# The delta-rule stage of a hybrid decoder step: 0/1 sums in two fp32r passes, zero-padded sample products, masks on the way out of PSUM, 32-row state updates

## The chip, the cores and the metric

The kernel runs on one core of a Trainium2 chip. The metric is the device time of one execution in microseconds; less is better. The times shown are medians of several runs of the same program.

## What is computed

One inference step of a decoder layer serves 256 prompt tokens of one request and 64 sample tokens (8 requests of 8 tokens). The layer is a mixer of 8 gated delta-rule heads and 4 retention heads, then attention over 256 memory tokens, then a gated feed-forward of 5632 hidden units; the model has 2048 features. All arrays are 32-bit floats. The change touches the delta-rule heads alone. For one head (keys and values of 128 features), in chunks:

```python
def gated_delta_chunked(q, k, v, g, beta, s0):
    # S_t = a_t S_{t-1} + b_t k_t (v_t - a_t S_{t-1}^T k_t)^T,  o_t = S_t^T q_t,  g = log a
    G = jnp.cumsum(g, -1)
    decay = jnp.exp(jnp.where(causal, G[..., :, None] - G[..., None, :], -jnp.inf))
    lower = jnp.where(strict, beta[..., :, None] * kk * decay, 0.0)        # kk = k k^T
    a_mat = lower + jnp.eye(C)
    rhs = jnp.concatenate([v * beta[..., None], k * (beta * jnp.exp(G))[..., None]], -1)
    sol = lax.linalg.triangular_solve(a_mat, rhs, left_side=True, lower=True, unit_diagonal=True)
    ...
    # per chunk: u = u_c - w_c S;  o = (q e^G) S + (qk * decay) u;  S = S e^{G_last} + (k e^{G_last - G})^T u
```

The prompt starts from a zero state; each of the 8 sample requests has a state of 128 x 128 of its own for every head, which is read, used and written back.

## The kernel before

The tokens are columns (256 of the prompt, 64 of the samples, 320 in all), and a weight tile of 128 x 128 is the stationary operand of TensorE. Every 32-bit weight and activation of a projection is cut into a high and a low fp32r part: ACT makes the high one (line 154, `hi`), VectorE the low one (line 155, `lo`), and TensorE adds three products of 320 columns (lines 234 to 236). The weights come in chunks of 1024 columns over SP's queue, four chunks ahead; a chunk is 24 such products. A product whose operands are not fp32r runs as fp32, which shows as two passes in the trace.

The projections are the bulk work. `weave(small, per)` runs a generator of small work beside it: each step of the generator (up to its `yield`) is queued behind a slice of bulk, and a slice asks for `per` nanoseconds of bulk times the yielded weight (2100 ns here, six groups of three products, or 18 products). The order of the instructions on each engine is written at compile time by the tile scheduler, from program order and its own estimate of when operands are ready; on the chip each engine takes its queue in that order.

The generator `gdn(hp)` treats two heads at a time, four pairs in all, each beside the projections of the next pair (the last beside the first retention head's). Its rows are five units of 128 tokens: two units of prompt tokens for each head, and one unit (number 4) with the 64 sample tokens of both heads. Its steps, with the lines of the profile:

- Line 511: `gin`, a triangle of ones times the log decays, on VectorE; it shares four slots (tag `t5`) with `DT`, `DM`, `Nt` and `Nm`. Line 542: inverse norms `r10` on POOL, then `vr` on VectorE (544).
- Lines 550 and 551: `pD` and `pC`, the sums of log decays between two tokens, as fp32 products of a 0/1 matrix with `gin`; ACT takes the exponent into `DT`, POOL masks it into `DM`.
- Lines 566 to 570: `pK` = k k^T and `pQ` = k q^T. Line 574: `pR`, sample keys and queries times the old states, in four column groups of 32; ACT copies it into `R` (580).
- Lines 577 and 578: `Nt` on VectorE. Then the inverse of the 8 x 8 diagonal blocks: `Nm` (583), `Nc` (585, a reduction) and `Z` (588) on VectorE; `pB` (592), a 0/1 product with `Z` on TensorE; 14 short instructions into `U8` (604, 605) and `U` (607) on VectorE.
- Line 597: `pS`, products of 0/1 selections `selK` and `selQ` with `R`, which bring the sample products to their rows.
- Line 612: POOL makes three masked copies `Ns` of `Nt`, one for each level of the blocked inverse (blocks of 8, 16 and 32).
- Lines 638 to 671, three levels: `pQ` from `Ns[i]` and `X`, ACT copies it into `Q` (640), `pU` (654), VectorE subtracts it from `U` (655), TensorE transposes `U` (669), ACT copies that into `X` (671).
- In between, the sample states: POOL scales the old states `S0` (646) and spreads `w` over the requests into `wm` (650); TensorE multiplies in four products of 64 rows and 512 columns (661); VectorE adds each to `S0` (663); SP stores the state.

Small products take their PSUM bank from a pool of four (`ps()`), the bulk from another four (`mm()`). SP's queue holds the weight loads, the state loads and the stores in program order.

Of the kernel before, what the change touches and what calls it, by code (L numbers as in the profile page):

```python
# [14 lines left out]
P = 128  # L15
# [3 lines left out]
NB = 8  # L19
# [25 lines left out]
def _constants():  # L45
# [14 lines left out]
    put("lvl", np.stack([(col // (2 * s) == row // (2 * s)) & (col // s > row // s) for s in (8, 16, 32)], 1))  # L60
# [5 lines left out]
    for name, q in (("selK", 0), ("selQ", 1)):  # L66
        s = np.zeros((P, 2, NS))
        for j in range(4):
            for par in range(2):
                for l in range(NL):  # L70
                    s[32 * j + 16 * q + 8 * par + l, par, NL * (2 * j + par) + l] = 1
        put(name, s)
# [32 lines left out]
def tile_hybrid_step(ctx: ExitStack, tc: tile.TileContext, I, O, gamma8):  # L105
# [63 lines left out]
    class Bulk:  # L169
        """The projections as one stream of tensor-engine work, drawn in slices."""  # L170
# [43 lines left out]
    def project(name, srcs, xs, evac, n=NT, kt=KT, banks=None, held=None, start=()):  # L214
        """srcs: weights [128, (k, 256)], two column tiles each; xs() gives (hi, lo) per 128 rows of K."""
# [68 lines left out]
    g5 = mc.tile([P, HP, 5], F32, name="g5")  # L284
    eG = mc.tile([P, HP, 5], F32, name="eG")
# [5 lines left out]
    def rstd_of(accs, width, n=NT):  # L291
        """1 / sqrt(mean over the partitions of the sum of accs + eps), tokens on partitions, one column per 128."""
# [108 lines left out]
    with tc.tile_pool(name="prep", bufs=1, side="right") as pp:  # L401
        xT = pp.tile([P, KT, NT], F32, name="xT")
        nc.sync.dma_start(gT, I["gains"])
        # pieces of x between the chunks of weights that meet them
# [16 lines left out]
        def prep():  # L421
            accs = [pp.tile([P, NT], F32, name=f"acc0{i}") for i in range(2)]
            for f in range(KT):
                o = pp.tile([P, NT], F32, tag="sq0", name="sq0", bufs=6) if f > 1 else accs[f]
                # behind the cuts that the tensor engine waits for
# [23 lines left out]
            # rows: tokens; the sample tokens twice, once per head of a pair  # L449
# [21 lines left out]
            dve.scalar_tensor_tensor(g5, ab, -1.0, al5[:, 0], op0=ALU.mult, op1=ALU.mult)  # L471
            gb = pp.tile([P, HP, 2 * NB], F32, name="gb")
# [28 lines left out]
    def gdn(hp):  # L501
# [8 lines left out]
        gin = gp.tile([P, 5, P], F32, tag="t5", name="gin", bufs=4)  # L510
        dve.tensor_tensor(gin[:, 0:4], bc(cc("triI").unsqueeze(1), [P, 4, P]), bc(g5[:, hp, 0:4].unsqueeze(2), [P, 4, P]), ALU.mult)
        dve.tensor_scalar(gin[:, 4], cc("triIC"), g5[:, hp, 4:5], None, op0=ALU.mult)
# [45 lines left out]
        kq = gp.tile([P, 2, 4, 2, 16], F32, tag="kq", name="kq")  # L558
        for h in range(2):
            for i, t in enumerate((k, q)):  # L560
                pool.tensor_copy(kq[:, h, :, i, :].rearrange("p j (b l) -> p j b l", b=2), t[:, 512 + h * NS : 512 + (h + 1) * NS].rearrange("p (j b l) -> p j b l", b=2, l=NL))
# [9 lines left out]
        pR = ps()  # L571
        for h in range(2):
            for j in range(4):
                pe.matmul(pR[32 * j : 32 * j + 32, h * NP : (h + 1) * NP], kq[:, h, j].rearrange("p i t -> p (i t)"), S0[h][:, 2 * j : 2 * j + 2, :], start=True, stop=True)
# [17 lines left out]
        pe.matmul(pB[:, :NT], cc("b8"), Z.rearrange("p u m c -> p (u m c)"), start=True, stop=True)  # L592
        pS = ps()
        for o, name in ((0, "selK"), (1, "selQ")):
            for h in range(2):
                for par in range(2):
                    pe.matmul(pS[h * NS : (h + 1) * NS, o * P : (o + 1) * P], cc(name)[:, par * NS : (par + 1) * NS], R[:, h, par], start=par == 0, stop=par == 1)
# [11 lines left out]
        Ns = []  # L609
# [7 lines left out]
        rh = gp.tile([P, 2, P], F32, tag="rh", name="rh")  # L617
        rhC = gp.tile([P, P], F32, tag="rhC", name="rhC")
        dve.scalar_tensor_tensor(rhC, un(pS, 0), nG[:, hp, 4:5], vr[:, 4], op0=ALU.mult, op1=ALU.add)
        qSC = gp.tile([P, P], F32, tag="qSC", name="qSC")  # L620
        act.activation(qSC, un(pS, 1), AF.Copy, scale=eG[:, hp, 4:5])
# [66 lines left out]
        def heads_out(lo, hi):  # L688
            """Head norm of every other unit."""
# [10 lines left out]
        def gates_out(lo, hi):  # L700
            """Back to features on partitions, gain and gate."""
# [10 lines left out]
        # prompt: two chunks from a zero state  # L712
# [54 lines left out]
    def ret(h):  # L767
# [8 lines left out]
        # sample keys and values with every group of 32 tokens four times: (high, low) of one meets (high, low) of the other  # L776
# [46 lines left out]
        # scores, transposed: keys on partitions  # L823
# [100 lines left out]
    def residual(name, w, xs, ssq, xg, gain, firsts=2):  # L924
        """x += W^T of the activations, for all columns; the next norm's inputs follow."""
# [414 lines left out]
```

## Time and profile before

| what | value |
| --- | --- |
| median of 3 runs | 2193.51 us (2192.74 to 2194.01) |
| span of the profiled execution, first to last instruction | 2192.0 us |
| instructions in the trace | 36250 |
| mean granted TensorE clock | 0.994 |
| stage of the delta-rule pairs | about 60 to 430 us |

The page gives the profiled execution by its span only; the timed runs lie 1.5 us above that span. Times in the rows are microseconds from the start of the span unless marked ns. A matmul is pipelined: its row shows a duration longer than the distance from its start to the next one's.

### The profile page before, as it was taken

How to read it: one execution, taken by the hardware profiler on the slowest of the kernel's cores; microseconds unless marked ns; L12 is line 12 of the kernel's file. 1: busy time of each engine (PE TensorE's matmuls, PEld its weight loads, DVE VectorE, ACT ScalarE, POOL GpSimd, SP SyncE). 2: the span in 40 equal slices, each digit the busy share in tenths (PEclk: the TensorE clock that was granted, in tenths of full speed). 3: DMA queues.
4: the chain of work that ended last, by engine and by line, in shares of the span. 5: the costliest groups of instructions: out<-in, count | busy, mean ns of one | idle time of the engine just before them, and what ended most of it. 6: DMA issues, size and time to landing. Idle time of an engine off the chain costs nothing.

```text
span 2192.0 us, 36250 instructions
## 1 busy us (share of the span) xinstructions
PE 2148.7 (98%) x14964; PEld 2062.4 (94%) x14964; DVE 1140.1 (52%) x1617; ACT 861.6 (39%) x1338; POOL 292.2 (13%) x326
## 2 busy tenths in 40 slices
PE   8899999999999999999999999999999999999997
PEld 7898988999999999788889999999999999999997
DVE  7667576465565644454455444444444443444455
ACT  6444434343345533344354333333233332333332
POOL 2324143111114100000001110000000000001011
PEclk9999999999999999999999999999999999999999
DMA  7343433365557545788865454545555445545543
GB/s 249 116 137 98 147 119 112 117 203 190 183 197 258 151 145 152 289 296 292 285 206 152 145 150 149 149 149 154 147 152 149 149 140 158 153 147 154 142 148 116
DMA packets 101974, 369.52 MB, mean 169 GB/s; under 512 B 11696, under 2 KB 12464, under 8 KB 99632
## 3 DMA queue, kind: packets, MB, share of 16 engines
q1 hardware_dynamic: 101808, 367.20, 53.0%
q8 instruction: 117, 1.92, 0.4%
q14 instruction: 49, 0.40, 0.1%
HBM read 345.85 MB, written 21.30 MB: 167 GB/s over the span
## 4 chain that ended last, share of the span: by engine, by line
PE 93%; DVE 3%; DMA 1%; ACT 1%; issue 1%; POOL 0%; SPq 0%; POOLq 0%; DVEq 0%; ACTq 0%
PE mm L234 22%; PE mm L236 22%; PE mm L235 22%; PE ps L236 5%; PE ps L234 5%; PE ps L235 5%; PE mm L979 1%; PE mm L981 1%; PE mm L980 1%; DVE lo L155 1%; PE ps L1130 1%; DMA Vs<-in_cache_mem_v_dram 1%; PE ps L661 1%; PE ps L1188 1%; PE ps L1173 1%
## 5 line engine op out<-in xcount | busy, mean ns | idle before, releaser
L234 PE MATMUL mm<-act,hi 128*128 128x320 f32 (+1 forms) x3456 | 1073.9, 311 | 5.9 <-ACT hi L154 5.9
L155 DVE TENSOR_TENSOR lo<-raw,hi 128x1024 fp32r<-128x1024 f32 (+1 forms) x561 | 687.6, 1226 | 728.6 <-ACT hi L154 725.5
L236 PE MATMUL mm<-act,lo 128*128 128x320 f32 (+1 forms) x3456 | 1063.3, 308 | 3.2 <-DVE lo L155 3.2
L235 PE MATMUL mm<-act,hi 128*128 128x320 f32 (+1 forms) x3456 | 1063.5, 308 | 1.4 <-DVE act L255 1.3
L154 ACT CAST hi<-raw 128x1024 fp32r<-128x1024 f32 (+1 forms) x561 | 579.7, 1034 | 871.8 <-PE mm L235 642.7
L234 PEld LDWEIGHTS mm<-act,hi 128*128 128x128 f32 x3456 | 651.0, 188 | 23.3 <-issue 15.4
L236 PEld LDWEIGHTS mm<-act,lo 128*128 128x128 f32 x3456 | 650.7, 188 | 7.2 <-DVE lo L155 4.4
L235 PEld LDWEIGHTS mm<-act,hi 128*128 128x128 f32 x3456 | 651.2, 188 | 4.8 <-issue 2.2
L236 PE MATMUL ps<-act,lo 128*128 128x320 f32 x704 | 217.7, 309 | 0.0
L235 PE MATMUL ps<-act,hi 128*128 128x320 f32 x704 | 217.6, 309 | 0.0
L234 PE MATMUL ps<-act,hi 128*128 128x320 f32 x704 | 217.6, 309 | 0.0
L1013 POOL TENSOR_TENSOR up<-up,ga 128x320 f32<-128x320 f32 x44 | 60.8, 1383 | 768.6 <-DVE up L1012 733.7
L236 PEld LDWEIGHTS ps<-act,lo 128*128 128x128 f32 x704 | 132.2, 188 | 0.0
L235 PEld LDWEIGHTS ps<-act,hi 128*128 128x128 f32 x704 | 132.2, 188 | 0.0
L234 PEld LDWEIGHTS ps<-act,hi 128*128 128x128 f32 x704 | 132.2, 188 | 0.0
L918 POOL TENSOR_TENSOR acc<-acc,sq 128x320 f32<-128x320 f32 x44 | 52.7, 1199 | 507.1 <-ACT sq L917 506.1
L249 ACT CAST act<-up 128x320 fp32r<-128x320 f32 x44 | 20.2, 460 | 96.9 <-POOL up L1013 96.9
L250 DVE TENSOR_TENSOR act<-up,act 128x320 fp32r<-128x320 f32 x44 | 21.7, 492 | 62.3 <-ACT act L249 62.3
L979 PE MATMUL mm<-hi,act 128*128 128x512 f32 x128 | 51.8, 405 | 0.0
L981 PE MATMUL mm<-hi,act 128*128 128x512 f32 x128 | 50.8, 397 | 0.0
L980 PE MATMUL mm<-lo,act 128*128 128x512 f32 x128 | 50.6, 395 | 0.0
L337 DVE SCALAR_TENSOR_TENSOR cy<-pre,cw,cy 128x344 f32<-128x344 f32 x72 | 46.6, 659 | 4.6 <-ACT cy L335 4.1
(334 smaller groups left out, 1450.0 us busy)
## 6 DMA issues: line engine op xcount, KB each, us to landing
raw<-in_w_in_dram SPq DMA_DIRECT2D x127, 512.0 KB, 3.9
raw<-in_w_gate_dram SPq DMA_DIRECT2D x88, 512.0 KB, 3.8
raw<-in_w_up_dram SPq DMA_DIRECT2D x88, 512.0 KB, 3.8
raw<-in_w_down_dram SPq DMA_DIRECT2D x80, 512.0 KB, 3.6
raw<-in_w_out_dram SPq DMA_DIRECT2D x32, 512.0 KB, 4.1
raw<-in_w_mem_q_dram SPq DMA_DIRECT2D x32, 512.0 KB, 3.9
raw<-in_w_mem_k_dram SPq DMA_DIRECT2D x32, 512.0 KB, 5.5
Kt<-in_cache_mem_k_dram SPq DMA_DIRECT2D x32, 512.0 KB, 7.0
```

The source lines that it names most:

```text
L154: act.copy(hi[:, :n], raw[:, :n])
L155: dve.tensor_tensor(lo[:, :n], raw[:, :n], hi[:, :n].bitcast(F32), ALU.subtract)
L234: pe.matmul(o, hi[:, w], xh[:, :n], start=g == 0, stop=False)
L235: pe.matmul(o, hi[:, w], xl[:, :n], start=False, stop=False)
L236: yield 3 * n / 2.4, pe.matmul(o, lo[:, w], xh[:, :n], start=False, stop=g == kt - 1)
L337: dve.scalar_tensor_tensor(cy[:, :CO], pre[:, i : i + CO], cw[:, i, ch : ch + 1], cy[:, :CO], op0=ALU.mult, op1=ALU.add)
L661: pe.matmul(pS, kd[r, 4], wm[r, 4 * half : 4 * half + 4].rearrange("p b v -> p (b v)"), start=True, stop=True)
L918: pool.tensor_tensor(self.accs[0], self.accs[0], sq, ALU.add)
L979: pe.matmul(pv[mt], xh[:, ms], hi[:, w], start=k0 + k == 0, stop=False)
L980: pe.matmul(pv[mt], xh[:, ms], lo[:, w], start=False, stop=False)
L981: yield 640.0, pe.matmul(pv[mt], xl[:, ms], hi[:, w], start=False, stop=k0 + k == KT - 1)
L1013: pool.tensor_tensor(u, u, sg[m], ALU.mult)
```

## The change

The edit is in `gdn` and in what prepares its constants:

- `gin` and `Z` are made twice, from a high and a low fp32r part of `g5` and of `Nc`, and `pD`, `pC` and `pB` become two accumulated fp32r products each with fp32r copies (`tri`) of the 0/1 matrices. `gin` has slots of its own.
- `kz` and `qz` hold the sample keys and queries with each group of eight columns in its place in a row of zeros, so that 32 accumulated products in four column groups write the sample products straight to their rows. `kq`, `pR`, `R`, `selK`, `selQ` and their products go.
- The level products take `Nt` unmasked; the level mask is applied when VectorE takes `pQ` out of PSUM into `Q`, which ACT copied before.
- The state update is made at level 2 in one step: four products of 32 rows and 512 columns into four PSUM banks, and sixteen VectorE instructions that scale the old state and add.

```diff
     put("strict", row > col)
-    put("lvl", np.stack([... & (col // s > row // s) for s in (8, 16, 32)], 1))
+    put("lvl", np.stack([... & (row // s > col // s) for s in (8, 16, 32)], 1))
...
+            act.copy(g5s[0], g5)
+            dve.tensor_tensor(g5s[1], g5, g5s[0].bitcast(F32), ALU.subtract)
+            for i, name in enumerate(("strict", "strictC", "b8")):
+                act.copy(tri[:, i], cc(name))
...
+    kz, qz = (gp.tile([P, 4, P], F32, name=n) for n in ("kz", "qz"))
+    pool.memset(kz, 0.0)
+    pool.memset(qz, 0.0)
...
-        gin = gp.tile([P, 5, P], F32, tag="t5", name="gin", bufs=4)
-        dve.tensor_tensor(gin[:, 0:4], ..., bc(g5[:, hp, 0:4].unsqueeze(2), [P, 4, P]), ALU.mult)
-        dve.tensor_scalar(gin[:, 4], cc("triIC"), g5[:, hp, 4:5], None, op0=ALU.mult)
+        gins = []
+        for g in g5s:
+            gin = gp.tile([P, 5, P], F32R, tag="gin", name="gin", bufs=2)
+            g = g.bitcast(F32)
+            dve.tensor_tensor(gin[:, 0:4], ..., bc(g[:, hp, 0:4].unsqueeze(2), [P, 4, P]), ALU.mult)
+            dve.tensor_scalar(gin[:, 4], cc("triIC"), g[:, hp, 4:5], None, op0=ALU.mult)
+            gins.append(gin)
+        for z, t in ((kz, k), (qz, q)):
+            s = t[:, 512 : 512 + P].rearrange("p (c b l) -> p c b l", b=4, l=NL)
+            pool.tensor_copy(z[:, :, 0:120].rearrange("p c (b x) -> p c b x", x=40)[:, :, :, 0:NL], s[:, :, 0:3])
+            pool.tensor_copy(z[:, :, 120:P], s[:, :, 3])
...
-        pe.matmul(pD, cc("strict"), gin[:, 0:4].rearrange("p u c -> p (u c)"), start=True, stop=True)
-        pe.matmul(un(pC, 0), cc("strictC"), gin[:, 4], start=True, stop=True)
+        for i, gin in enumerate(gins):
+            pe.matmul(pD, tri[:, 0], gin[:, 0:4].rearrange("p u c -> p (u c)"), start=i == 0, stop=i == 1)
+        for i, gin in enumerate(gins):
+            pe.matmul(un(pC, 0), tri[:, 1], gin[:, 4], start=i == 0, stop=i == 1)
...
-        kq = gp.tile([P, 2, 4, 2, 16], F32, tag="kq", name="kq")
-        (four pool.tensor_copy of k and q into kq)
...
-        pR = ps()
-        for h in range(2):
-            for j in range(4):
-                pe.matmul(pR[32 * j : 32 * j + 32, h * NP : (h + 1) * NP], kq[:, h, j]..., S0[h][:, 2 * j : 2 * j + 2, :], ...)
+        pS = ps()
+        for i, z in enumerate((kz, qz)):
+            for b in range(4):
+                for c in range(4):
+                    pe.matmul(pS[32 * c : 32 * c + 32, i * P : (i + 1) * P], z[:, c, 32 * b : 32 * b + 32], S0[c // 2][:, 4 * (c % 2) + b, :], start=b == 0, stop=b == 3)
...
-        act.copy(R.rearrange("p h a v -> p (h a v)"), pR)
+        act.activation(qSC, un(pS, 1), AF.Copy, scale=eG[:, hp, 4:5])
...
-        dve.tensor_tensor(Z, bc(Nc.unsqueeze(2), [P, 5, NL, NL]), bc(d8.unsqueeze(1), [P, 5, NL, NL]), ALU.mult)
+        Ns = split(Nc.rearrange("p u c -> p (u c)"), None, 5 * NL, dst=[...])
+        for t in Ns:
+            Z = gp.tile([P, 5, NL, NL], F32R, tag="Z", name="Z", bufs=2)
+            dve.tensor_tensor(Z, bc(t.bitcast(F32)..., [P, 5, NL, NL]), bc(d8.unsqueeze(1), [P, 5, NL, NL]), ALU.mult)
+            Zs.append(Z)
+        dve.scalar_tensor_tensor(rhC, un(pS, 0), nG[:, hp, 4:5], vr[:, 4], op0=ALU.mult, op1=ALU.add)
         yield 1.5
...
-        pe.matmul(pB[:, :NT], cc("b8"), Z.rearrange("p u m c -> p (u m c)"), start=True, stop=True)
-        pS = ps()
-        (eight pe.matmul of selK and selQ with R into pS)
+        for i, Z in enumerate(Zs):
+            pe.matmul(pB[:, :NT], tri[:, 2], Z.rearrange("p u m c -> p (u m c)"), start=i == 0, stop=i == 1)
...
-        for i in range(3):
-            t = gp.tile([P, 4, P], F32, tag="Ns", name="Ns", bufs=3)
-            pool.tensor_tensor(t, Nt[:, 0:4], bc(lv(i).unsqueeze(1), [P, 4, P]), ALU.mult)
-            Ns.append(t)
...
             for u in range(4):
-                pe.matmul(un(pQ, u), Ns[i][:, u], X[:, u], start=True, stop=True)
+                pe.matmul(un(pQ, u), Nt[:, u], X[:, u], start=True, stop=True)
             Q = gp.tile([P, 4, P], F32, tag="Q", name="Q")
-            act.copy(Q, g4(pQ))
+            dve.tensor_tensor(Q, g4(pQ), bc(lv(i).unsqueeze(1), [P, 4, P]), ALU.mult)
             if i == 0:
...
-                for h in range(2):
-                    pool.tensor_tensor(S0[h], S0[h], bc(eTC[:, hp, h * NB : (h + 1) * NB].unsqueeze(2), [P, NB, P]), ALU.mult)
-                wm = gp.tile([P, NB, P], F32, tag="wm", name="wm")
-                (two pool.tensor_tensor of 64 rows into wm)
+                wm = gp.tile([P, 4, P], F32, tag="wm", name="wm")
+                pool.tensor_tensor(wm, bc(w[:, 4].unsqueeze(1), [P, 4, P]), bc(cc("blkq").unsqueeze(2), [P, 4, P]), ALU.mult)
+            if i == 2:
+                pSs = [ps() for _ in range(4)]
+                for c in range(4):
+                    r = slice(32 * c, 32 * c + 32)
+                    pe.matmul(pSs[c], kd[r, 4], wm[r].rearrange("p b v -> p (b v)"), start=True, stop=True)
+                for c in range(4):
+                    for b in range(4):
+                        j = 4 * (c % 2) + b
+                        sv = S0[c // 2][:, j]
+                        dve.scalar_tensor_tensor(sv, sv, eTC[:, hp, c // 2 * NB + j : c // 2 * NB + j + 1], un(pSs[c], b), op0=ALU.mult, op1=ALU.add)
+                    if c % 2:
+                        nc.sync.dma_start(O["state_gdn_sample"][2 * hp + c // 2], S0[c // 2])
             yield
...
-            if i > 0:
-                for half in range(2):
-                    ...
-                    pe.matmul(pS, kd[r, 4], wm[r, 4 * half : 4 * half + 4].rearrange("p b v -> p (b v)"), start=True, stop=True)
-                    sv = S0[h][:, 4 * half : 4 * half + 4]
-                    dve.tensor_tensor(sv, sv, g4(pS), ALU.add)
-                nc.sync.dma_start(O["state_gdn_sample"][2 * hp + h], S0[h])
             yield
```

## Rows read from the trace of the kernel before

**Rows 1.** The page, part 1: busy time, share of the span, instructions.

```profile
PE 2148.7 (98%) x14964; PEld 2062.4 (94%) x14964; DVE 1140.1 (52%) x1617; ACT 861.6 (39%) x1338; POOL 292.2 (13%) x326
```

**Rows 2.** TensorE's waits, 60 to 430 us: us in total, times, longest.

```profile
PE ps L592 <- DVE Z L588: 13.1, 4, 4.7
...
PE ps L669 <- DVE U L655: 0.6, 1, 0.6
```

**Rows 3.** Stages: from:to and length, busy of each engine, PEclk, DMA share, GB/s.

```profile
99.30:106.00 6.70, 6.21 (x29) 5.02 (x30) 3.70 (x13) 1.31 (x2) 0.08 (x1) 0.50 0.18 70
...
191.50:198.10 6.60, 5.64 (x27) 4.44 (x28) 6.53 (x15) 1.95 (x4) 4.49 (x5) 0.50 0.23 67
...
287.00:290.30 3.30, 3.30 (x21) 2.38 (x20) 3.30 (x3) 0.00 (x0) 3.02 (x4) 0.50 0.00 0
...
378.10:386.00 7.90, 6.82 (x52) 5.95 (x53) 7.45 (x18) 1.42 (x2) 3.90 (x2) 1.00 0.22 66
```

**Rows 4.** Timeline of TensorE, pair 1: start, us, line, count [idle before <- releaser].

```profile
181.76 1.05 PE L566 MATMUL ps<-post 128*128 128x128 f32 x8
...
184.08 1.07 PE L574 MATMUL ps<-S,kq 128*32 128x256 f32 x16
185.08 0.42 PE L234 MATMUL mm<-act,hi 128*128 128x320 f32 x1
...
192.46 1.44 PE L592 MATMUL ps<-Z,cst 128*128 128x320 f32 x2 [3.57 <-DVE Z L588]
...
198.28 0.31 PE L234 MATMUL mm<-act,hi 128*128 128x320 f32 x1
198.43 0.31 PE L235 MATMUL mm<-act,hi 128*128 128x320 f32 x1
```

**Rows 5.** Timeline of TensorE, pair 3.

```profile
378.09 0.81 PE L592 MATMUL ps<-Z,cst 128*128 128x320 f32 x2 [1.32 <-DVE Z L588]
378.82 1.15 PE L597 MATMUL ps<-R,cst 128*64 128x128 f32 x16
379.90 0.42 PE L234 MATMUL mm<-act,hi 128*128 128x320 f32 x1
```

**Rows 6.** Timeline of VectorE, pair 1.

```profile
184.15 1.11 DVE L577 SCALAR_TENSOR_TENSOR Nt<-ps,b,DT 128x128 f32<-128x128 f32 x4
185.19 0.67 DVE L615 TENSOR_TENSOR qkd<-ps,DM 128x512 f32<-128x512 f32 x1
```

**Rows 7.** The chain of work that ended last: start, us, engine, line, count.

```profile
126.46 1.91 PE ps L661 x4
...
178.20 0.86 PE ps L550 x2
...
186.31 1.07 DVE Nm L583
187.38 1.70 DVE gin L511
189.08 1.22 DVE Nc L585
...
190.55 1.87 DVE Z L588
```

**Rows 8.** Timeline of POOL, pair 1.

```profile
185.40 4.80 POOL L612 TENSOR_TENSOR Ns<-Nt,cst 128x512 f32<-128x512 f32 x3 [1.27 <-DVE Nt L577]
```

**Rows 9.** Lines, 60 to 430 us: busy us, mean ns | idle before <- releaser.

```profile
L655 DVE TENSOR_TENSOR U<-U,ps 128x512 f32<-128x512 f32 x12 | 8.2, 683 | 11.0 <-PE ps L654 11.0
L348 DVE TENSOR_TENSOR z<-mm,rB 128x320 f32<-128x320 f32 x8 | 3.9, 486 | 3.1 <-PE mm L236 3.1
L607 DVE TENSOR_TENSOR U<-U,cst 128x640 f32<-128x640 f32 x4 | 3.3, 824 | 0.1
L340 ACT ACTIVATE post<-cy 128x64 f32<-128x64 f32 x20 | 4.8, 242 | 0.0
```

**Rows 10.** One line, 60 to 430 us: ns min/median/max, first and last start.

```profile
L155 DVE TENSOR_TENSOR lo<-raw,hi x69: 1204/1225/2846, 60.7 to 426.3; 128x1024 fp32r<-128x1024 f32 x69
```

More of the change, by code (lines that the diff above doesn't have):

```diff
@@ L59, in _constants @@
     put("strict", row > col)
-    put("lvl", np.stack([(col // (2 * s) == row // (2 * s)) & (col // s > row // s) for s in (8, 16, 32)], 1))
+    put("lvl", np.stack([(col // (2 * s) == row // (2 * s)) & (row // s > col // s) for s in (8, 16, 32)], 1))
     put("triIC", same & (row <= col))
@@ L65, in _constants @@
     put("d8", np.repeat(row % NL == np.arange(NL)[None, :], NL, axis=1))
-    for name, q in (("selK", 0), ("selQ", 1)):
-        s = np.zeros((P, 2, NS))
-        for j in range(4):
[L69 to L72, printed above, removed]
     put("blk", row // NL == np.arange(2 * NB)[None, :])
@@ L284, in tile_hybrid_step @@
     g5 = mc.tile([P, HP, 5], F32, name="g5")
+    g5s = [mc.tile([P, HP, 5], F32R, name=f"g5{x}") for x in "hl"]
+    tri = mc.tile([P, 3, P], F32R, name="tri")
     eG = mc.tile([P, HP, 5], F32, name="eG")
@@ L509, in gdn @@
             S0.append(s)
-        gin = gp.tile([P, 5, P], F32, tag="t5", name="gin", bufs=4)
-        dve.tensor_tensor(gin[:, 0:4], bc(cc("triI").unsqueeze(1), [P, 4, P]), bc(g5[:, hp, 0:4].unsqueeze(2), [P, 4, P]), ALU.mult)
-        dve.tensor_scalar(gin[:, 4], cc("triIC"), g5[:, hp, 4:5], None, op0=ALU.mult)
+        gins = []
+        for g in g5s:
+            gin = gp.tile([P, 5, P], F32R, tag="gin", name="gin", bufs=2)
+            g = g.bitcast(F32)
+            dve.tensor_tensor(gin[:, 0:4], bc(cc("triI").unsqueeze(1), [P, 4, P]), bc(g[:, hp, 0:4].unsqueeze(2), [P, 4, P]), ALU.mult)
+            dve.tensor_scalar(gin[:, 4], cc("triIC"), g[:, hp, 4:5], None, op0=ALU.mult)
[4 more added lines that the diff above has]
+            pool.tensor_copy(z[:, :, 120:P], s[:, :, 3])
         t1, t2, t3, t4 = ps(), ps(), ps(), ps()
@@ L570, in gdn @@
         pe.matmul(un(pC, 1), un(k, 4), un(q, 4), start=True, stop=True)
-        pR = ps()
-        for h in range(2):
-            for j in range(4):
-                pe.matmul(pR[32 * j : 32 * j + 32, h * NP : (h + 1) * NP], kq[:, h, j].rearrange("p i t -> p (i t)"), S0[h][:, 2 * j : 2 * j + 2, :], start=True, stop=True)
+        pS = ps()
[3 more added lines that the diff above has]
+                    pe.matmul(pS[32 * c : 32 * c + 32, i * P : (i + 1) * P], z[:, c, 32 * b : 32 * b + 32], S0[c // 2][:, 4 * (c % 2) + b, :], start=b == 0, stop=b == 3)
         Nt = gp.tile([P, 5, P], F32, tag="t5", name="Nt", bufs=4)
@@ L578, in gdn @@
         dve.scalar_tensor_tensor(Nt[:, 4], un(pC, 0), b2[:, 4:5], DT[:, 4], op0=ALU.mult, op1=ALU.mult)
-        R = gp.tile([P, 2, 2, P], F32, tag="R", name="R")
-        act.copy(R.rearrange("p h a v -> p (h a v)"), pR)
+        rh = gp.tile([P, 2, P], F32, tag="rh", name="rh")
+        rhC = gp.tile([P, P], F32, tag="rhC", name="rhC")
+        qSC = gp.tile([P, P], F32, tag="qSC", name="qSC")
+        act.activation(qSC, un(pS, 1), AF.Copy, scale=eG[:, hp, 4:5])
         Nm = gp.tile([P, 5, P], F32, tag="t5", name="Nm", bufs=4)
@@ L585, in gdn @@
         dve.tensor_reduce(Nc, Nm.rearrange("p u (b c) -> p u c b", c=NL), op=ALU.add, axis=AX.X)
-        Z = gp.tile([P, 5, NL, NL], F32, tag="Z", name="Z")
+        Ns = split(Nc.rearrange("p u c -> p (u c)"), None, 5 * NL, dst=[gp.tile([P, 5 * NL], F32R, tag=f"Ns{x}", name="Ns") for x in "hl"])
+        Zs = []
         d8 = cc("d8").rearrange("p (m c) -> p m c", c=NL)
-        dve.tensor_tensor(Z, bc(Nc.unsqueeze(2), [P, 5, NL, NL]), bc(d8.unsqueeze(1), [P, 5, NL, NL]), ALU.mult)
+        for t in Ns:
+            Z = gp.tile([P, 5, NL, NL], F32R, tag="Z", name="Z", bufs=2)
+            dve.tensor_tensor(Z, bc(t.bitcast(F32).rearrange("p (u c) -> p u c", c=NL).unsqueeze(2), [P, 5, NL, NL]), bc(d8.unsqueeze(1), [P, 5, NL, NL]), ALU.mult)
+            Zs.append(Z)
+        dve.scalar_tensor_tensor(rhC, un(pS, 0), nG[:, hp, 4:5], vr[:, 4], op0=ALU.mult, op1=ALU.add)
         yield 1.5
         pB = ps()
-        pe.matmul(pB[:, :NT], cc("b8"), Z.rearrange("p u m c -> p (u m c)"), start=True, stop=True)
-        pS = ps()
[L594 to L597, printed above, removed]
+        for i, Z in enumerate(Zs):
+            pe.matmul(pB[:, :NT], tri[:, 2], Z.rearrange("p u m c -> p (u m c)"), start=i == 0, stop=i == 1)
         NB8 = pB[:, :NT].rearrange("p (u m c) -> p u m c", m=NL, c=NL)
@@ L616, in gdn @@
         dve.tensor_tensor(qkd[:, 4], un(pC, 1), DM[:, 4], ALU.mult)
[L617 to L621, printed above, removed]
         yield 1.5
```

12 lines of the change are left out of this document (1 added, 11 removed).

## Prediction

> **What bounds the kernel now.** First the busy times of the page [rows 1]: TensorE is busy for 98% of the span and VectorE for 52%, so a change pays where TensorE waits, runs slowly or has less to do. That share hides two losses, idle pieces and a low clock, and the reader is to see both in the delta-rule stage, about 60 to 430 us, where the bulk work (the next projection) could otherwise run through.
>
> Next the list of TensorE's waits in that stage [rows 2]: of all its idle time, 13.1 us in four pieces, one for each pair of heads, stands ahead of one product, pB (line 592), and ends with VectorE's Z (line 588). Last the table of stages, cut to the stretches after these four [rows 3]. After three of the waits TensorE ran at half clock (granted 0.50, so 1.2 GHz): 6.21, 5.64 and 3.30 us of its work. After the fourth, 1.32 us long [rows 5], it stayed at 1.00. At half clock half of such time is lost: (6.21 + 5.64 + 3.30) / 2 = 7.6 us. So the chain to Z costs 13.1 + 7.6 = 20.7 us now, and how long that chain becomes is the main question.
>
> **The chain to Z, in pair 1.** TensorE starts pK (line 566) at 181.76 and stands ready for pB 3.57 us before 192.46, that is 7.13 us after pK's start [rows 4]. VectorE starts Nt at 184.15, 2.39 us after pK's start [rows 6]; Nm follows at 186.31, 2.16 us later, and the chain goes on with 1.07 for Nm, 1.70 for a gin that belongs to the next pair, 1.22 for Nc and 1.87 for Z [rows 7]. Beside it POOL runs three Ns products for 4.80 us without a pause [rows 8], then scales S0. VectorE's instructions are drawn out there: Nm and U (line 607) both make 640 elements of two SBUF inputs, and U takes 0.82 [rows 9]; Z makes 320, and z (line 348) takes 0.49 for as many; a weight cut takes 1.23 in the median and up to 2.85 [rows 10].
>
> **The change, part by part, for each of four pairs.**
>
> *The chain.* Removed: Ns and the scaling of S0 from POOL, so what is left on it beside this chain is small copies. gin has slots of its own and no longer waits for one of the four that it shared with DT, DM, Nt and Nm; both new gins can go while VectorE idles ahead of vr, so I take 1.70 out of the chain. Added: an ACT copy of Nc (0.24 as for 64 columns [rows 9], with 0.05 for each of two handovers, from Z's end at 192.42 to pB at 192.46), a subtraction that I price no higher than that copy, and a second Z. New length: 2.16 + 0.82 + 1.22 + 0.24 + 0.10 + 0.24 + 2 x 0.49 = 5.76. At each dependence VectorE's queue may hold something else, and I count one cut, 1.23: 6.99, ending 2.39 + 6.99 = 9.38 after pK's start. TensorE arrives at 7.13 + 0.83 (more work, below) = 7.96. Wait 1.42, four times 5.7: **saved 7.4**. Bounds: no cut, wait 0.2 (saved 12.3); a cut of 2.85, wait 3.04 (saved 0.9).
>
> Nc stays at its 1.22: whether it too was drawn out no row tells, since all four ran beside POOL; by Nm's ratio (0.82 to 1.07) it would be 0.94. The Trainium skill (SBUF — State Buffer, Who interferes with whom) says that a VectorE instruction with two SBUF inputs contends with a GpSimd instruction that reads SBUF, and that a reduction never does. By that rule Nc keeps its 1.22; by Nm's ratio the four waits would shrink by another 1.1 us together.
>
> *The clock.* A wait of 1.42 lies nearest to the 1.32 after which the clock stayed up; falls are shown from 3.57. So I take all of it: **saved 7.6** (bounds 0 and 7.6).
>
> *TensorE's work.* An fp32r product of 320 columns follows the one before after 0.15 [rows 4], so 0.235 for 512 (estimate by columns).
> - pD: 0.86 [rows 7] becomes 2 x 0.235, saves 0.39. pC: two products of 128 columns at fp32r where there was one of fp32; by columns 0.12 in place of 0.22, by a rate no better than fp32's 0.44. I take no change.
> - pB: from 378.09 to 378.82, 0.73 [rows 5], becomes 2 x 0.15, saves 0.43.
> - Sample products: pR took 1.00 (184.08 to 185.08 [rows 4]) for 16 passes of 256 columns, so four ran at once; the selections took 1.08 [rows 5]. New are 64 passes of 128 columns in the same four column groups: four at once, at 0.11 a round (a quarter of the 0.43 of 512 columns in pD), is 16 x 0.11; pR's four rounds of 256 columns would be 0.86 at that rate and took 1.00, so something goes to the start, of which I add half: 1.83. Saves 0.25; it stands 0.83 longer ahead of pB and 1.08 shorter behind it.
> - State updates: 2 x 1.91 [rows 7] for eight passes of 512 columns, 0.43 each. New: eight such passes, of 32 rows each, into four banks. No row shows row groups at once; bounds are one at a time, 8 x 0.43 + 0.1 = 3.55, and four at once as the column groups of pR, 0.96. The four banks are all that the pool of small products has, and pQ still holds one, so the last quarter waits for Q: three at once and one behind, 4 x 0.43 = 1.75, saves 2.07 (0.27 to 2.86).
>
> Together 0.39 + 0.43 + 0.25 + 2.07 = 3.14, four times: **saved 12.6** (4.5 to 16.2, with pC's ends). The Trainium skill (TensorE: Matmul & The Clock Gate, Part 3, Measured speedup vs the span model) gives 3.07 times for four row tiles of 32 rows and 512 columns, which as an estimate makes 3.55 into 1.16 if a bank were free.
>
> *New waits.* (1) Q now comes from VectorE (0.68, as U's subtraction [rows 9]) in place of ACT. That subtraction stands in just such a place, twelve times, and made TensorE wait 0.6 in all [rows 2]; so 0.6 for twelve Qs. (2) The last quarter of the update needs Q done: 0.68 and up to one cut in progress, 1.23, against 0.96 of the other three; about 0.5, 2 in all. Bulk products are queued behind it on TensorE. (3) Sixteen scalar_tensor_tensor of 128 columns, four in 1.04 from the first's start to the next instruction's [rows 6], so 4.2, in place of four additions of 512 (2.7), and U's subtraction queues behind them: 4.2 + 0.68 + one cut 1.23 = 6.1. Its cover is the update (1.75), two slices of bulk (18 products of 0.15 each, 5.4 together) and little more, near 7; with a second cut some 0.5 is short, 2 in all. Without that cover it is rival 2. Together **lost 4.6** (0 to 10). The two state stores wait for this burst in SP's queue, with weight loads behind them; four loads run ahead, 24 products of 0.15 or 3.6 us of bulk each, so nothing. The masks of Q replace POOL's, kz and qz replace the kq copies on POOL ahead of the pair, as short. wm is one POOL product of 512 elements in place of two of 1024. The splits in the first stage are some six instructions under 0.3 us, behind the projection; uncovered 1.5.
>
> Sum: 7.4 + 7.6 + 12.6 - 4.6 = 23.0. The page gives the profiled execution its span, 2192.0; the timed runs lie 1.5 above it, so 2193.5 - 23.0 = **2170.5**, said as 2170.
>
> **The rivals.**
> 1. *The chain stays as long* (fillers take the place of gin). Waits and clock as before: 12.6 - 4.6 = 8.0 saved, 2185.5. For it: every dependence on VectorE had a filler. Against: Z alone loses 1.4 when POOL is quiet. 0.14.
> 2. *VectorE's burst holds the banks.* All four small banks wait for it. 6.1 less 1.75 is 4.35 of wait for each pair, 17.4: 2170.5 + 17.4 - 2.0 (item 3, already counted) = 2185.9; it also decides the sign if the clock falls each time (2.8, half of 5.64: 11.3 more, 2197). For it: TensorE's order was set at compile time. Against: two slices of bulk stand behind the update. The Trainium skill (TensorEngine Tiling (Array Packing), PSUM Bottleneck) warns of just this, that evacuation does not get faster with the tiles. 0.10, a quarter of it without a gain.
> 3. *The chain grows, and the kernel is slower.* Both Zs drawn out to 1.87 by POOL copies and the cut to 2.85: 2.39 + 5.76 + 2.85 + 2 x 1.38 = 13.76, wait 5.8, four times 23.2; the clock falls in all four pairs, 4 x 2.8 = 11.3. That is 34.5 for 20.7 now: 13.8 lost, 8.0 saved by the rest, 2199.3. It ends slower from 12.4 us more than now. Against: POOL has little left there. 0.06.
> 4. *No effect*: what TensorE gains is waited for elsewhere, at weights or cuts, which already use VectorE. Against: TensorE's waits in the stage name hardly any [rows 2]. 0.05, 2190 to 2194.
>
> **How the numbers follow.** My forecast holds 0.61, from 2160 to 2180; better than that 0.04. Rivals 1 and 2 reach to 2187. Under 2160 and over 2187 together some 0.18 is left out, so the range is 2160 to 2187. A measurement tells 0.2%, 4.4 us, from no change. Faster: 0.61 + 0.04 + 0.14 + 0.08 = 0.87. Same: 0.05 and a little of rival 2, 0.06. Slower: 0.07.
>
> **What the profile after would show.** pB waits under 2 us in each pair, and a clock of 1.00 in all stages to 430 us; the weight cuts of that stretch mostly near 1.23; the update's passes started together in groups and its TensorE time near 1.8; no wait of TensorE over 1 us for Q, for the sixteen additions or for a bank. Wrong would be the forecast if Z still ends later than 3 us after TensorE arrives (rival 1 or 3), or if a new wait behind line 660 exceeds 2 us a pair (rival 2).

## The result, and the profile after

The changed kernel takes 2169.1 us (median of 4 runs, 2166.61 to 2169.94) beside 2193.21 for the kernel before in the same rounds: a ratio of 0.9887 (95% interval 0.9873 to 0.9901). The forecast was 2170. The profiled execution took 2169.4 us with a span of 2167.3, so the span is 24.7 us shorter.

The page's busy times answer to [rows 1]: POOL does 49 us less, TensorE 16 us less, VectorE the same.

```profile
PE 2133.0 (98%) x15092; PEld 2058.3 (95%) x15092; DVE 1138.3 (53%) x1694; ACT 854.8 (39%) x1330; POOL 243.4 (11%) x304
```

The list of TensorE's waits, 55 to 430 us (us in total, times, longest), answers to [rows 2]. pB is now line 612 and Z line 605: 13.1 us in four pieces have become 3.9 in three.

```profile
PE ps L612 <- DVE Z L605: 3.9, 3, 2.4
PE ps L576 <- DVE vr L556: 1.6, 1, 1.6
PE ps L565 <- ACT jk L536: 1.2, 3, 0.4
PE ps L579 <- DVE vr L556: 0.9, 1, 0.9
PE ps L658 <- DVE Q L646: 0.5, 1, 0.5
PE ps L633 <- DVE U L622: 0.4, 1, 0.4
```

TensorE's timeline (start, us, line, count, wait ahead) answers to [rows 4, 5]. Rows at 168 to 186 and 212 to 216 us belong to pair 1, those at 125 to 127 to pair 0, those at 356 to pair 3.

```profile
125.14 1.98 PE L658 MATMUL ps<-wm,kd 32*128 32x512 f32 x8
127.05 0.42 PE L227 MATMUL mm<-act,hi 128*128 128x320 f32 x1
...
168.08 0.63 PE L563 MATMUL ps<-gin,tri 128*128 128x512 f32 x2
168.64 0.44 PE L565 MATMUL ps<-gin,tri 128*128 128x128 f32 x2
168.92 0.36 PE L227 MATMUL mm<-act,hi 128*128 128x320 f32 x1
...
171.61 1.16 PE L576 MATMUL ps<-post 128*128 128x128 f32 x8
...
174.04 1.08 PE L586 MATMUL ps<-S,kz 128*32 128x128 f32 x32
...
175.92 0.41 PE L227 MATMUL mm<-act,hi 128*128 128x320 f32 x1
...
182.08 0.84 PE L612 MATMUL ps<-Z,tri 128*128 128x320 f32 x2 [2.37 <-DVE Z L605]
182.74 0.45 PE L227 MATMUL mm<-act,hi 128*128 128x320 f32 x1
182.98 0.47 PE L228 MATMUL mm<-act,hi 128*128 128x320 f32 x1
183.25 0.47 PE L229 MATMUL mm<-act,lo 128*128 128x320 f32 x1
...
212.84 1.13 PE L658 MATMUL ps<-wm,kd 32*128 32x512 f32 x6
214.47 1.12 PE L658 MATMUL ps<-wm,kd 32*128 32x512 f32 x2 [0.50 <-DVE Q L646]
215.52 0.42 PE L227 MATMUL mm<-act,hi 128*128 128x320 f32 x1
...
356.67 0.46 PE L612 MATMUL ps<-Z,tri 128*128 128x320 f32 x2
356.96 0.31 PE L227 MATMUL mm<-act,hi 128*128 128x320 f32 x1
```

Work is read from one start to the next. The state update takes 1.91 us (125.14 to 127.05) where it took 2 x 1.91; the sample products 1.88 where pR and the selections took 1.00 + 1.08; pB 0.29 in pair 3 where it took 0.73, but 0.66 in pair 1 (182.08 to 182.74), where its second product waits for the second Z; pD 0.56 and pC 0.28. After the one wait of 2.37 us the bulk products follow each other at 0.27 in place of 0.15: half clock. The table of stages for that stretch answers to [rows 3], where there were three such, with 15.15 us of TensorE's work in them.

```profile
182.90:186.10 3.20, 3.20 (x14) 3.20 (x13) 2.71 (x11) 2.54 (x4) 1.40 (x4) 0.50 0.43 151
```

VectorE's timeline in pair 1 answers to [rows 6] and to the chain in [rows 7].

```profile
171.73 2.13 DVE L148 TENSOR_TENSOR lo<-raw,hi 128x1024 fp32r<-128x1024 f32 x1
...
174.19 0.68 DVE L518 TENSOR_TENSOR gin<-cst,g5h 128x512 fp32r<-128x512 f32 x1
...
175.78 1.11 DVE L589 SCALAR_TENSOR_TENSOR Nt<-ps,b,DT 128x128 f32<-128x128 f32 x4
...
177.88 0.81 DVE L597 TENSOR_TENSOR Nm<-Nt,cst 128x640 f32<-128x640 f32 x1
178.72 1.41 DVE L599 TENSOR_REDUCE Nc<-Nm 128x40 f32<-128x640 f32 x1
180.03 0.35 DVE L607 SCALAR_TENSOR_TENSOR rhC<-ps,nG,vr 128x128 f32<-128x128 f32 x1
180.28 1.23 DVE L148 TENSOR_TENSOR lo<-raw,hi 128x1024 fp32r<-128x1024 f32 x1
181.42 0.21 DVE L243 TENSOR_TENSOR Ns<-Nc,Ns 128x40 fp32r<-128x40 f32 x1
181.53 0.90 DVE L605 TENSOR_TENSOR Z<-Ns,cst 128x320 fp32r<-128x320 f32 x2
...
214.33 4.21 DVE L663 SCALAR_TENSOR_TENSOR S<-S,eTC,ps 128x128 f32<-128x128 f32 x16
219.36 0.69 DVE L670 TENSOR_TENSOR U<-U,ps 128x512 f32<-128x512 f32 x1 [0.81 <-PE ps L669]
```

Of POOL's larger work one piece is left beside the chain of pair 1, the mask DM, which runs ahead of Nt:

```profile
171.51 1.27 POOL L570 TENSOR_TENSOR DM<-DT,cst 128x512 f32<-128x512 f32 x1 [0.68 <-ACT DT L567]
172.74 1.44 POOL L571 TENSOR_TENSOR DM<-DT,cst 128x128 f32<-128x128 f32 x1
```

Nm takes 0.81 for the 1.07 of [rows 7], the two Zs take 0.90 together, and one cut of 1.23 stands between Nc and the split. The two gins (1.59 from 174.19 to 175.78) and a cut of 2.13, beside POOL's DM, stand ahead of Nt. The sixteen additions take 4.21, and U is subtracted without TensorE waiting.

### The profile page after: what moved, and what is told of

The parts are those of the page before. It is cut to its first block, busy times and chain, and to the rows that moved or that the text cites. A ratio compares the mean times of both kernels' runs of the same rounds, so it can differ in the third digit from the quotient of the medians.

```text
span 2167.3 us, 36521 instructions
## 1 busy us (share of the span) xinstructions
PE 2133.0 (98%) x15092; PEld 2058.3 (95%) x15092; DVE 1138.3 (53%) x1694; ACT 854.8 (39%) x1330; POOL 243.4 (11%) x304
## 4 chain that ended last, share of the span: by engine, by line
PE 93%; DVE 3%; issue 1%; DMA 1%; ACT 1%; POOL 0%; SPq 0%; POOLq 0%; DVEq 0%; ACTq 0%
PE mm L227 22%; PE mm L229 22%; PE mm L228 22%; PE ps L227 5%; PE ps L229 5%; PE ps L228 5%; PE mm L985 1%; PE mm L987 1%; PE mm L986 1%; PE ps L1136 1%; DMA Vs<-in_cache_mem_v_dram 1%; DVE lo L148 1%; PE ps L1194 1%; PE ps L1179 1%; PE ps L669 1%
## 5 line engine op out<-in xcount | busy, mean ns | idle before, releaser
L227 PEld LDWEIGHTS mm<-act,hi 128*128 128x128 f32 x3456 | 650.7, 188 | 18.5 <-issue 10.4
L1028 DVE TENSOR_TENSOR xR<-xR,mm 128x320 f32<-128x320 f32 x48 | 23.2, 484 | 47.8 <-PE mm L229 47.8
```

The source lines that it names most:

```text
L227: pe.matmul(o, hi[:, w], xh[:, :n], start=g == 0, stop=False)
L1028: dve.tensor_tensor(x, x, pm[:, :NT], ALU.add)
```

## The experiments

**The theory.** Most of the gain comes from POOL: what it did beside the chain drew out VectorE's instructions, so pB waited and the clock fell; the shorter state update gives the rest. **The rivals:** the fp32r passes and the sample products matter as much, because TensorE has less to do; or only the place of the bulk work mattered, and more of it ahead of pB would have done the same.

**a_pool.** The changed kernel, with POOL's old work beside the chain put back. Its results go to a spare tile that nothing reads.

```
+        for i in range(3):
+            t = gp.tile([P, 4, P], F32, tag="junk", name="junk", bufs=1)
+            pool.tensor_tensor(t, Nt[:, 0:4], bc(lv(i)...), ALU.mult)
...
+                for h in range(2):
+                    for e in range(2):
+                        t = gp.tile([P, 4, P], F32, tag="junk", name="junk", bufs=1)
+                        pool.tensor_tensor(t, S0[h][:, 4 * e : 4 * e + 4], bc(eTC[...]...), ALU.mult)
```

> The changed kernel with POOL's old work put back beside the chain to Z: three masked products of Nt and four products of half an old state each, written to a spare tile that nothing reads. The outputs are the same. Theory (POOL's work made the chain long): the cut, Nm and the two Zs are drawn out again as before the change, the four waits ahead of pB go from 3.9 us to some 10 to 15 us in all, the clock falls in two or three pairs, and the time is 2178 to 2188 us. Rival (the gain is TensorE's fewer passes): nothing on TensorE changes, so the time stays within 3 us of 2169.

Measured: 2186.53 us, 0.9967 (0.9956 to 0.9978), that is 17.4 us of the 24.1 given back. The waits of its TensorE, and VectorE's timeline in pair 1:

```profile
PE ps L612 <- DVE Z L605: 14.4, 7, 4.9
...
PE ps L636 <- DVE U L622: 1.6, 1, 1.6
```

```profile
182.52 1.08 DVE L597 TENSOR_TENSOR Nm<-Nt,cst 128x640 f32<-128x640 f32 x1
183.64 1.35 DVE L599 TENSOR_REDUCE Nc<-Nm 128x40 f32<-128x640 f32 x1
...
185.17 2.01 DVE L148 TENSOR_TENSOR lo<-raw,hi 128x1024 fp32r<-128x1024 f32 x1
187.10 1.03 DVE L243 TENSOR_TENSOR Ns<-Nc,Ns 128x40 fp32r<-128x40 f32 x1
188.05 1.73 DVE L605 TENSOR_TENSOR Z<-Ns,cst 128x320 fp32r<-128x320 f32 x2
```

Beside them POOL is busy without a pause:

```profile
181.63 4.46 POOL L626 TENSOR_TENSOR junk<-Nt,cst 128x512 f32<-128x512 f32 x3 [2.80 <-DVE Nt L589]
186.17 5.65 POOL L657 TENSOR_TENSOR junk<-S,eTC 128x512 f32<-128x512 f32 x4
```

The same instructions as in the changed kernel's pair 1 take 1.08 for 0.81 (Nm), 2.01 for 1.23 (the cut), 1.03 for 0.21 (the split), 1.73 for 0.90 (the Zs); the reduction Nc, 1.35 for 1.41, is not drawn out. Work that nobody needs, on an engine busy for 13% of the span, costs 17 us. The terms account for it in the profiled executions, which lie 17.1 us apart: Z's wait 10.5 more, U's 1.2 more, and half clock in three stretches with 3.25, 6.19 and 4.67 us of TensorE's work where there was one of 3.20, 5.5 more. The theory's first half is shown.

**b_pool.** The kernel before with the two parts that take work off POOL, the level masks and the state update; old sums, old sample products, old slots of gin.

```
...
-            pool.tensor_tensor(t, Nt[:, 0:4], bc(lv(i)...), ALU.mult)
...
-                pe.matmul(un(pQ, u), Ns[i][:, u], X[:, u], start=True, stop=True)
+                pe.matmul(un(pQ, u), Nt[:, u], X[:, u], start=True, stop=True)
-            act.copy(Q, g4(pQ))
+            dve.tensor_tensor(Q, g4(pQ), bc(lv(i)...), ALU.mult)
...
-                    pool.tensor_tensor(S0[h], S0[h], bc(eTC[...]...), ALU.mult)
+                pSs = [ps() for _ in range(4)]
+                for c in range(4):
+                    pe.matmul(pSs[c], kd[r, 4], wm[r]..., start=True, stop=True)
+                        dve.scalar_tensor_tensor(sv, sv, eTC[...], un(pSs[c], b), ...)
...
```

> The kernel before with the two parts of the change that take work from POOL: level masks on the way out of PSUM, and the state update in 32-row products with the scaling in VectorE's additions. Still fp32 sums, old sample products with selections, gin in the shared slots. Theory: the waits ahead of pB go from 13.1 to 4 to 7 us and the clock stays up in most pairs, 12 us or so, and the update itself gives 6.6 (as 15.3 to 8.7 us of TensorE's time in the traces), so 2173 to 2178 us. Rival (the gain is TensorE's fewer passes): the update alone, about 2187 us. Rival (gin's own slots shorten the chain): gin stays between Nm and Nc, the waits stay over 9 us, 2183 or more.

Measured: 2166.12 us (2164.65 to 2166.9), 0.9876 (0.9863 to 0.9889): better than I expected, and all of the change's gain. Its wait for Z, and gin on VectorE in pair 1:

```profile
PE ps L592 <- DVE Z L588: 1.4, 2, 0.8
```

```profile
176.53 0.68 DVE L511 TENSOR_TENSOR gin<-cst,g 128x512 f32<-128x512 f32 x1
```

The clock does not fall in the stage. Z's waits 13.1 - 1.4 = 11.7, U's waits 1.7 (1.1 and 0.6, here none), clock 7.6 and the update 15.3 - 8.7 = 6.6 make 27.6, for 27.4 us gained. gin still stands between Nm and Nc, as in the kernel before, but takes 0.68 us for the 1.70 of [rows 7]: most of its cost there came with POOL's work beside it.

**b_masks, b_state, b_sample.** One part each on the kernel before: the first and the second half of b_pool's edit, and the sample products alone:

```
-                pe.matmul(pR[32 * j : 32 * j + 32, ...], kq[:, h, j]..., S0[h][:, 2 * j : 2 * j + 2, :], ...)
+                    pe.matmul(pS[32 * c : 32 * c + 32, ...], z[:, c, 32 * b : 32 * b + 32], S0[c // 2][:, 4 * (c % 2) + b, :], start=b == 0, stop=b == 3)
...
-                    pe.matmul(pS[...], cc(name)[...], R[:, h, par], start=par == 0, stop=par == 1)
```

> The kernel before with one part of the change alone: the level masks are applied by VectorE when Q is taken out of PSUM, so POOL no longer makes Ns; POOL still scales S0 and spreads wm over 64 rows. Theory (POOL's work beside the chain to Z makes it long): half of POOL's work there goes, 4.7 of some 9 us, and it is the half that meets Nm, so the waits ahead of pB and U go from 14.2 to 6 to 9 us, with one or two half-clock stretches fewer, 2180 to 2187 us. Rival (only both together matter, as S0's scaling moves up into the place of Ns): within 4 us of 2193.5.

> The kernel before with the other part alone: the state update in four 32-row products and sixteen scaling additions on VectorE; POOL still makes Ns, no longer scales S0, and spreads wm once. Theory: 6.6 us of TensorE's update time, and the late half of POOL's work (which meets the cut and Z) gone, waits from 14.2 to 7 to 10 us, 2175 to 2183 us. Rival (VectorE's sixteen additions in a row delay U and the cuts): 2187 or more.

> The kernel before with the zero-padded sample products alone: no kq, R and selections. POOL keeps Ns and S0. Theory: TensorE does 0.2 to 0.3 us less work in each pair, 0.8 us longer of it ahead of pB and 1.1 shorter behind it, so the wait moves from pB to U by as much and nothing is won but that, 2190 to 2194 us. Rival (the work ahead of pB shortens the waits, 0.8 in each pair and with it the clock): 2183 to 2188 us.

Measured: b_masks 2188.45, 0.9979 (0.9970 to 0.9988), a little worse than expected; b_state 2173.57, 0.9914 (0.9901 to 0.9928), a little better; b_sample 2193.39, 1.0003 (0.9995 to 1.0012). Z's wait in the three: 9.6, 6.7 and 7.2 us. In b_sample it did not go away but moved behind pB, as its list shows:

```profile
PE ps L598 <- DVE Z L593: 7.2, 3, 3.0
PE ps L624 <- DVE U L608: 6.3, 4, 2.2
PE ps L650 <- ACT Q L636: 2.9, 1, 2.9
```

Masks and state alone gain 4.6 and 18.9 us, in sum 23.5, and together 27.4; the 3.9 between is no more than these intervals (2 to 3 us each) leave open. The granted clock shows half speed in two stretches for b_masks, in one for b_state and in none for both.

**b_rows and b_scale.** The state part cut in two: only the 32-row products (POOL still scales S0), or only the scaling moved into the additions (products of 64 rows as before).

```
b_rows  +                    pe.matmul(pSs[c], kd[r, 4], wm[r]..., start=True, stop=True)
        +                    dve.tensor_tensor(sv, sv, g4(pSs[c]), ALU.add)
b_scale -                    pool.tensor_tensor(S0[h], S0[h], bc(eTC[...]...), ALU.mult)
        +                        dve.scalar_tensor_tensor(sv, sv, eTC[...], un(pS, e), op0=ALU.mult, op1=ALU.add)
```

> The kernel before with the 32-row products of the state update alone: four products in four row groups at level 2, four additions of 512 columns as before; POOL still makes Ns and scales S0 beside the chain to Z, and spreads wm once instead of twice. Theory (two separate gains in the state part): TensorE's update time falls by 6.6 us in all, the waits ahead of pB stay at 10 to 13 us with their half clock, 2185 to 2188 us. Rival (the 18.9 us that the whole state part gave come from the row groups and the new place): 2173 to 2178 us.

> The kernel before with the scaling of the old states moved from POOL into VectorE's additions, four of 128 columns for each of 512, and nothing else: products of 64 rows, two at each of levels 1 and 2, wm as before. TensorE does the same work. Theory (POOL's scaling beside the chain to Z is what this part takes away): the waits ahead of pB fall to 5 to 9 us, two of three half-clock stretches go, 2180 to 2184 us. Rival (the chain is not helped): 2191 to 2196 us.

Measured: b_rows 2185.2, 0.9966 (0.9954 to 0.9979), with Z's wait at 13.1 as before and the update at 7.75 us for 15.3; b_scale 2182.6, 0.9953 (0.9940 to 0.9967), with Z's wait at 6.8 and the update at 15.3. Two separate effects, 7.8 and 10.4 us, in sum 18.2, make up b_state's 18.9. What the clock costs, b_rows shows to be in part a matter of the execution. Its four waits for Z are those of the kernel before (4.67, 3.58, 3.57 and 1.32), but half clock followed only the first two, with 6.8 us of work in place of 15.15; after the third, which halved the clock in the kernel before, it stayed up:

```profile
279.85 0.81 PE L592 MATMUL ps<-Z,cst 128*128 128x320 f32 x2 [3.57 <-DVE Z L588]
```

```profile
279.80:283.20 3.40, 3.35 (x28) 2.74 (x29) 3.40 (x4) 0.00 (x0) 3.40 (x5) 1.00 0.00 0
```

**b_slack25 and a_slack25.** One number, in the kernel before and in the changed one: more bulk work ahead of pB.

```
-        yield 1.5
+        yield 2.5
```

> The kernel before with one number changed: the step ahead of pB yields 2.5 in place of 1.5, so 2100 ns more of bulk is queued ahead of pB in each pair. The chain and POOL stay as they are. Theory (TensorE runs out of queued work while Z is made, and its clock falls after that): the waits shrink by some 2.6 us in each of three pairs, 13.1 to 4 us or less, the clock stays at 1.00, 2174 to 2180 us. Rival (the bulk that is moved ahead is missing later in the stage): other waits appear, 2188 to 2194 us.

> The changed kernel with the same one number, 2.5 in place of 1.5 ahead of pB. Theory: the 3.9 us of waits ahead of pB and the 1.7 us that one stretch at half clock costs go, 2163 to 2166 us. Rival (bulk is missing later): 2168 to 2171 us.

Measured: b_slack25 2193.96, 1.0003 (0.9995 to 1.0012). Here the theory missed by 14 us and the rival was right:

```profile
PE ps L628 <- DVE U L607: 7.6, 3, 3.8
PE ps L592 <- DVE Z L588: 5.4, 2, 2.7
```

The wait moved to the next product that depends on VectorE: 13.0 us in sum, with half clock in four stretches (15.3 us of TensorE's work in them). This reads as VectorE's time over the whole stretch setting the pace, and not the place of the bulk in it. a_slack25 came to 2166.57, 0.9881 (0.9867 to 0.9894), between what theory and rival expected: Z's wait is gone and U's is 2.1, and the time is within the interval of the changed kernel.

**a_fp32 and a_noz.** The changed kernel without its fp32r passes (single fp32 gin, Z, pD, pC and pB), and with only Z and pB single.

```
...
a_fp32  -            pe.matmul(pD, tri[:, 0], gin[...], start=i == 0, stop=i == 1)
        +        pe.matmul(pD, cc("strict"), gin[...], start=True, stop=True)
both    -            pe.matmul(pB[:, :NT], tri[:, 2], Z..., start=i == 0, stop=i == 1)
        +        pe.matmul(pB[:, :NT], cc("b8"), Z..., start=True, stop=True)
```

> The changed kernel with the two fp32r passes undone: one fp32 gin (in one slot of its own) and one fp32 Z, pD, pC and pB as before; the three other parts stay. Theory from the traces so far: TensorE works some 3.3 us longer on pD and pB, and the chain to Z loses the ACT copy, the subtraction, one Z and one gin, so the waits ahead of pB (3.9 us) and the one half-clock stretch (1.7) mostly go: 2164 to 2169 us, no slower than the changed kernel. Rival (the passes are worth what they save on TensorE): 2172 to 2175 us.

> The changed kernel with one fp32 Z and one fp32 pB again (no split of Nc on ACT and VectorE); the two gins and their fp32r products stay. If the split ahead of Z is what the fp32r part pays with: the waits ahead of pB fall from 3.9 to under 1.5 us and no stretch at half clock is left before 430 us; pB costs 1.7 us more on TensorE; 2164 to 2168 us. If it is the second gin: waits stay at 3 to 4 us and the time goes up by the 1.7, 2170 to 2172 us.

Measured: a_fp32 2166.52, 0.9883 (0.9868 to 0.9898); a_noz 2167.24, 0.9884 (0.9871 to 0.9898). Z's wait falls from 3.9 to 0.3 and 1.1, U's grows from 0.4 to 2.2 and 2.7, and the clock stays up in both. What the fp32r passes save on TensorE comes back as a longer chain: nothing measurable in the end. The fp32r passes alone on the kernel before were not tried, nor slots of its own for gin alone.

**after_again.** The changed kernel once more, for the spread and the clock.

> The changed kernel once more, unchanged, on the chip of these runs, for the comparison with its parts. 2167 to 2170 us.

Measured: 2168.09, 0.9888 (0.9874 to 0.9901). TensorE's timeline in pair 1 shows nearly the same wait without a fall of the clock:

```profile
181.87 0.82 PE L612 MATMUL ps<-Z,tri 128*128 128x320 f32 x2 [2.33 <-DVE Z L605]
182.53 0.31 PE L227 MATMUL mm<-act,hi 128*128 128x320 f32 x1
182.67 0.31 PE L228 MATMUL mm<-act,hi 128*128 128x320 f32 x1
```

Its profiled execution took 2167.83 us, 1.6 less than the other, which is half of that one's 3.20 us at half clock.

No version is clearly faster than the changed kernel: b_pool, a_slack25 and a_fp32 lie 2 to 3 us below it (1.5 to 2 below its second measurement), inside the intervals.

## Why the prediction was right

The mechanism was right: without POOL's work the chain is shorter, the waits and the half clock mostly go, and the update is cheaper. That the time was met to 1.4 us is partly luck, since mis-sized terms cancel: by the measurements below, chain +1.8, clock -1.6, TensorE's work -2.7 and new waits +5.3 us.

- **Chain, saved 7.4: measured 9.2** (13.1 to 3.9). The waits were 0.76, 2.37, 0.77 and 0 where 1.42 each was forecast. In pair 1 TensorE arrived 8.10 us after pK's start (7.96 forecast), and Nt to the end of the Zs took 6.65 (6.99 with its one cut); the wait ends with the first Z, where the forecast took the second. The step that failed is the start: both gins were to go "while VectorE idles ahead of vr", but in pair 1 they stood ahead of Nt, behind a cut drawn out to 2.13 beside POOL's DM, where the forecast had left POOL only "small copies". Nt began 4.17 us after pK's start, not 2.39. In pairs 0 and 2 half of the work for gin did go ahead of vr (it starts at 85.16 and 258.57), and pair 3, with no next pair and so no gin, had no wait. The 1.70 taken out for gin was mostly POOL's doing, as b_pool's 0.68 in the old place shows.
- **Nc at its 1.22: measured 1.31** in the same reading (178.72 to 180.03; the 1.22 is its part of the chain). Its row took 1.29 in the kernel before, 1.41 here, and 1.35 beside a busy POOL in a_pool: POOL does not draw it out. That agrees with the Trainium skill (SBUF — State Buffer, Who interferes with whom), by which a reduction never contends. It also agrees that two-input instructions do, with the sizes that a_pool shows.
- **Clock, saved 7.6: measured 6.0.** One stretch of 3.20 us at 0.50 was left, 1.6 lost. The place was not foreseen: "falls are shown from 3.57" held for the trace of before, but here one followed 2.37. b_rows and after_again show that the size of this term is partly chance: the same waits cost 7.6 us in one execution and 3.4 in another, or 1.6 and nothing.
- **TensorE's work, saved 12.6: measured 9.9**, from the starts of the four pairs. The update gave 6.6 (15.3 to 8.7, with the 0.5 wait for Q in it; forecast 8.3): 1.91 a pair for 1.75 where nothing waited (by its own 0.43 the forecast's four passes are 1.72). Three groups at once and one behind was the right picture. pB fell short too: 0.44 saved in pair 3 for 0.43 forecast, but 0.08 in each of pairs 1 and 2, where the second product waits for the second Z (0.66 for 0.73), so 0.9 in all for 1.7. The sample products gave 0.20 a pair for 0.25, and pD 1.8 in all for 1.56, without the waits for jk that stand beside it; pC lost 0.2 in all where no change was taken.
- **New waits, lost 4.6: far less came.** Q cost 0.5 once, already in the update (1.0 in all beside b_state's 7.75, where Q came from ACT); the sixteen additions took 4.21 as counted and nobody waited for them. Other waits changed little: vr 2.1 to 2.5, U 1.7 to 0.4, jk 1.0 to 1.2.

By these the stage gains 9.2 + 6.0 + 9.9 + 0.7 = 25.8; the first retention transposes, which end it, start 25.9 us earlier (455.88 to 429.94). The splits in the first stage, priced at 1.5 if uncovered, cost nothing: the first pD starts at 82.16 where it started at 82.31. The span is 24.7 shorter, so some 1.2 us are lost behind the stage; 0.9 of them is one wait of TensorE for the attention's keys from DMA (`Kt`), 0.2 us before and 1.1 after.

Of the signs named ahead, two failed in pair 1 alone: pB waited 2.37 and not under 2, and the clock stood at 0.50 for 3.20 us. The update took 1.91 in two pairs, and 2.68 and 2.25 in pairs 1 and 2, where its last part came later. The cuts (1.23 in the median, 2.13 at most) and the absence of new waits over 1 us came as said.

What the sum did not show is what each part is worth. I credited the fp32r passes and the sample products with 4.3 us of the 12.6 (0.39 + 0.43 + 0.25 for each pair). b_sample and a_fp32 show that this is worth nothing here: it makes TensorE arrive earlier at a wait for VectorE. And taking work from POOL is worth more than its waits, because half clock goes with them: b_scale waits 6.3 us less for Z and is 10.4 us faster, with half clock in two stretches for three.

Rivals 1 and 3 needed the chain to stay or grow; a_pool shows that it does so with POOL's work, and that this work has gone. Rival 2 fell: no wait of TensorE for the additions shows in its list, with two slices of bulk behind the update. Rival 4 holds for two parts of the change and not for the whole.

## What to carry to other kernels

An engine that is busy for a tenth of the span and off the critical path can still set the time, if its instructions run beside VectorE's on that path: read the duration of the same instruction with and without that neighbour. A saving on TensorE ahead of a wait for VectorE is no saving, nor is more bulk work put there: ask what the next dependence will wait for. A wait also costs the clock that falls after it, and that cost comes and goes in pieces: three stretches at half clock before, two without the masks on POOL, one without the scaling and with the new update, none with both, in the profiles here. Whether a wait of 2 to 3.6 us costs one differed between executions here, so give that term a range from nothing to the whole.

## What the runs showed of the hardware

- POOL's work draws out VectorE's two-input instructions in SBUF: 0.81 to 1.08 for 640 columns, 1.23 to 2.01 for 1024, 0.21 to 1.03 for 40. A reduction of 640 columns took 1.35 to 1.41 either way.
- Two waits of nearly one length in two executions of one kernel, 2.37 and 2.33 us: half clock for 3.20 us after the first, full clock after the second. Over all profiles of this stage, no wait of TensorE under 1.6 us was followed by work at half clock and every one from 3.8 us was; between them both occur (half after 2.19 in b_state, full after 2.81 in b_masks and 3.57 in b_rows).
- Two fp32r products of 128 columns took 0.28 us (pC), no less than the one fp32 product before (0.24, 84.38 to 84.62). With 320 columns two took 0.29 with no wait ahead (pB, pair 3), where the fp32 product took 0.63 with none (b_pool, 353.07 to 353.70) and 0.73 behind one.
- Eight passes of 32 rows and 512 columns took 1.91 us, where one alone takes 0.43 and one at a time would be 3.4: row groups do run at once, three of them here, with the fourth waiting for its bank. The Trainium skill (TensorE: Matmul & The Clock Gate, Part 3, Measured speedup vs the span model) gives 3.07 times for four; these runs show 3.4 / 1.91 = 1.8 times for three and one behind, and no run here had four banks free.
